# The latent feed-forward of a diffusion trunk by seven products of quarters, in two phases

## The chip, the cores and the metric

The kernel runs on one core of a Trainium2 chip. What is measured is the time of one execution on the device in microseconds (us). TensorE (PE) multiplies matrices from SBUF into PSUM, with weight loads (PEld) beside it; VectorE (DVE), ScalarE (ACT) and GpSimd (POOL) do the elementwise work; SyncE (SP) issues most DMA transfers, in one queue in order.

## What is computed

Two layers over 1024 latent tokens of 1024 features and 256 context tokens. Each layer has attention and pooling, an output projection with a layer norm, and then this feed-forward, whose result is added to the scaled input and normed again:

```python
def conv_ffn(h, w_up, conv_w, conv_b, w_down):
    u = h @ w_up
    L = u.shape[1]
    half = CONV_WIDTH // 2
    up = jnp.pad(u, ((0, 0), (half, half), (0, 0)))
    acc = up[:, 0:L] * conv_w[0] + conv_b
    for j in range(1, CONV_WIDTH):
        acc = acc + up[:, j:j + L] * conv_w[j]
    a, g = jnp.split(acc, 2, axis=-1)
    return (a * jax.nn.silu(g)) @ w_down

ffn = conv_ffn(x * (1 + s2) + sh2, w_up[l], conv_w[l], conv_b[l], w_down[l])
x = layer_norm(DEEPNORM_ALPHA * x + g2 * ffn, ln2_g[l], ln2_b[l])
```

All inputs are float32. In layer 0 the context tokens run the same feed-forward on their own; in layer 1 they don't.

## The kernel before

Every float32 operand of a large product is split into two float32r parts, a high one (a cast on ScalarE, `h`) and the rest (a subtraction on VectorE, `lo`). A product is three matmuls: high by high, high by low, low by high. A matmul here has 128 rows of contraction, 128 output rows and 512 columns. `wunit` (L149 on) loads 512 KB of weights into one of three `raw` buffers, casts (L156) and subtracts (L158).

The latent feed-forward is `ffn` (L1138 on) with the input `mixs`, which holds high and low parts of the tokens as `[128, 8 token tiles, 8 feature blocks, 128]`. It works on pairs f = 0 to 21 of blocks of 128 hidden features: `pair(f)` computes block f and block 22 + f. For one block `up` makes 2 halves of the tokens x 8 feature blocks x 3 = 48 matmuls (L1110). So there are 44 x 48 = 2112 matmuls a layer in the up product. `conv` (L1158 on) reads the block in PSUM: one activation on ScalarE for the middle tap, two `scalar_tensor_tensor` on VectorE for the others (L1163, L1166). Then SiLU on ScalarE (L1184), the gate as a product on GpSimd (L1185), and the split of the gated values.

The gated values stay in SBUF. After every two pairs (the list `G24`) `down` multiplies them by their rows of `w_down`, for 8 token tiles x 2 halves of the columns x 3 matmuls a pair (L1205), 1056 matmuls a layer in all. Before that GpSimd multiplies the raw weights by the gate vector `g2` (L154). VectorE adds each group's result into `acc` (L1216), a tile of 128 x 8 x 1024 in SBUF. `residual` (L1222 on) adds the scaled input in between: two products on GpSimd (L1226, L1227) and one `scalar_tensor_tensor` on VectorE (L1228). With the last group each token tile is normed (`ln_add`) and passed on by `tail`.

In layer 0 the background of the pairs also computes the next layer's modulation: 48 loads of 512 KB, each reduced by one VectorE instruction (L167). The first pair's products run ahead of the loop (`ups_before`), under the end of the output projection or of the context's feed-forward.

The program is written in this order, and a scheduler then sets the order of the instructions on each engine by its own estimate of times; each engine works off its row in order. PSUM is one pool of four tiles of 128 x 1024.

## Time and profile before

| what | value |
| --- | --- |
| median of 2 runs | 3015.48 us (3013.93 to 3017.04) |
| span of the profiled execution | 3008.6 us |
| TensorE matmuls | busy 2913.8 us (97%) |
| VectorE | busy 1872.5 us (62%) |
| ScalarE | busy 1261.9 us (42%) |
| GpSimd | busy 832.5 us (28%) |
| L1110, up, latent tokens | three groups of 1408 matmuls, 439 us each |
| L1205, down | three groups of 792 matmuls (264 of the 2376 belong to the context), 247 to 249 us each |
| DMA | 370.0 MB, 123 GB/s in the mean |

The span runs from the first to the last instruction on the core; the runs are timed from outside. Busy time is the union of the instructions of a group. Matmuls overlap one another, so the mean duration of one (389 ns) is not the distance between two; that distance comes out of a chain or a stretch. "Idle before" in a group is what the engine waited for ahead of it, and it costs something only on the engine that sets the end.

### The profile page before, as it was taken

Reading aid. Unit: us, or ns where it says so; the run is one execution under the profiler, and the core shown is the slowest. Engines: PE = TensorE matmul, PEld = TensorE weight load, DVE = VectorE, ACT = ScalarE, POOL = GpSimd, SP = SyncE. Lnnn points to the kernel's source line nnn. Section 1 sums busy time; section 2 is a strip of 40 time slices with the busy share of each in tenths; the row PEclk is TensorE's granted clock in tenths of the full one; section 3 lists DMA queues with packets and bytes.
Section 4 is the critical chain, followed back from the end, with each engine's and each line's share of the span. In section 5 each row is a group of like instructions: output and inputs, shape, how many; then the busy total and the mean of one; then the engine's idle time right before and its main releaser. Section 6 shows DMA issues by size and latency. Waiting matters only on the chain. (4 is left out here: it accounts for less than half of the span.)

```text
span 3008.6 us, 40753 instructions
## 1 busy us (share of the span) xinstructions
PE 2913.8 (97%) x15507; PEld 2477.8 (82%) x15507; DVE 1872.5 (62%) x3146; ACT 1261.9 (42%) x1980; POOL 832.5 (28%) x668
## 2 busy tenths in 40 slices
PE   8998889999999999999999999999999999999998
PEld 6798778977887888888888789888878888888886
DVE  5975789936886655556445754799845354444445
ACT  4223888834554322222223423798733322222223
POOL 0204363122532312121202632343222221212213
PEclk9999999999999999999999999999999999999999
DMA  7886652154554433332221654642133111211211
GB/s 282 246 271 188 186 162 89 36 175 164 177 187 155 159 98 98 106 111 91 84 63 64 211 191 141 176 126 87 57 117 112 57 50 49 63 56 56 70 46 60
DMA packets 186790, 370.00 MB, mean 123 GB/s; under 512 B 17290, under 2 KB 101346, under 8 KB 186084
## 3 DMA queue, kind: packets, MB, share of 16 engines
q1 hardware_dynamic: 185300, 363.11, 38.2%
q10 hardware_dynamic: 1296, 4.29, 0.4%
q8 instruction: 123, 2.02, 0.3%
q14 instruction: 71, 0.58, 0.1%
HBM read 303.46 MB, written 63.89 MB: 122 GB/s over the span
## 5 line engine op out<-in xcount | busy, mean ns | idle before, releaser
L158 DVE TENSOR_TENSOR wl<-raw,wh 128x1024 fp32r<-128x1024 f32 (+1 forms) x244 | 320.5, 1318 | 471.0 <-ACT wh L156 468.2
L156 ACT CAST wh<-raw 128x1024 fp32r<-128x1024 f32 (+1 forms) x250 | 258.2, 1037 | 824.2 <-PE u L1110 564.0
L1110 PE MATMUL u<-mxh,wh 128*128 128x512 f32 x1408 | 439.1, 390 | 2.6 <-DVE xtnl L163 1.5
L1110 PE MATMUL u<-mxl,wh 128*128 128x512 f32 x1408 | 439.0, 389 | 0.1
L1110 PE MATMUL u<-mxh,wl 128*128 128x512 f32 x1408 | 438.7, 389 | 0.0
L1110 PEld LDWEIGHTS u<-mxh,wh 128*128 128x128 f32 x1408 | 264.1, 188 | 58.1 <-DVE xtnl L163 1.7
L1110 PEld LDWEIGHTS u<-mxl,wh 128*128 128x128 f32 x1408 | 264.3, 188 | 55.6 <-DVE mxl L163 0.5
L1110 PEld LDWEIGHTS u<-mxh,wl 128*128 128x128 f32 x1408 | 264.3, 188 | 54.8
L154 POOL TENSOR_TENSOR raw<-raw,g 128x1024 f32<-128x1024 f32 x66 | 162.0, 2458 | 494.4 <-DMA raw<-in_wdown_dram 288.2
L163 DVE TENSOR_TENSOR PT<-pt,PT 128x512 fp32r<-128x512 f32 (+2 forms) x396 | 247.8, 644 | 17.4 <-ACT PT L162 14.9
L1205 PE MATMUL d<-wl,fh 128*128 128x512 f32 x792 | 249.1, 395 | 8.7 <-DVE wl L158 8.3
L1205 PE MATMUL d<-wh,fh 128*128 128x512 f32 x792 | 246.6, 395 | 2.7 <-ACT wh L156 1.3
L755 PE MATMUL s<-K,q 128*128 128x256 f32 (+2 forms) x960 | 235.5, 358 | 12.8 <-DVE m L722 11.2
L1205 PE MATMUL d<-wh,fl 128*128 128x512 f32 x792 | 247.7, 393 | 0.0
L1185 POOL TENSOR_TENSOR cv<-cv 128x1024 f32<-128x1024 f32 (+1 forms) x63 | 125.1, 1987 | 411.8 <-ACT cv L1184 411.8
L763 ACT ACTIVATE P<-P,m 128x1280 f32<-128x1280 f32 (+3 forms) x216 | 221.9, 1028 | 7.4 <-DVE m L722 6.4
L162 ACT CAST PT<-pt 128x512 fp32r<-128x512 f32 (+2 forms) x396 | 205.3, 558 | 24.2 <-PE pt L803 10.5
L817 PE MATMUL pvs<-PT,V 128*128 128x256 f32 (+1 forms) x1488 | 209.1, 288 | 5.1 <-DVE PT L163 2.0
L1216 DVE TENSOR_TENSOR acc<-d,acc 128x1024 f32<-128x1024 f32 x144 | 173.4, 1218 | 60.0 <-PE d L1205 59.9
L722 DVE CUSTOM_DVE_ANT_0 P<-s,zero,m 128x512 f32<-128x512 f32 (+1 forms) x288 | 189.0, 656 | 19.1
L299 PE MATMUL pacc<-wh,mxh 128*128 128x512 f32 (+1 forms) x512 | 189.4, 370 | 7.1 <-DVE rt L265 2.8
L817 PEld LDWEIGHTS pvs<-PT,V 128*128 128x128 f32 x1488 | 185.5, 190 | 11.8 <-ACT mixr L828 4.2
(237 smaller groups left out, 5449.2 us busy)
## 6 DMA issues: line engine op xcount, KB each, us to landing
raw<-in_wup_dram SPq DMA_DIRECT2D x132, 512.0 KB, 3.6
wm<-in_wmT_dram SPq DMA_DIRECT2D x96, 512.0 KB, 4.1
raw<-in_wdown_dram SPq DMA_DIRECT2D x66, 512.0 KB, 3.8
q<-QN SPq DMA_DIRECT2D x96, 128.0 KB, 3.3
q<-QG SPq DMA_DIRECT2D x96, 128.0 KB, 2.8
VD<-stB SPq DMA_DIRECT2D x20, 512.0 KB, 3.1
KD<-kt SPq DMA_DIRECT2D x20, 512.0 KB, 3.5
K<-KD SPq DMA_DIRECT2D x16, 640.0 KB, 5.0
```

The lines of the kernel that those rows point to most:

```text
L156: nc.scalar.copy(h[:, :n], raw[:, :n])
L158: (sub or nc.vector).tensor_tensor(out=lo[:, :n], in0=raw[:, :n], in1=h[:, :n], op=ALU.subtract)
L162: nc.scalar.copy(h, src)
L163: nc.vector.tensor_tensor(out=lo, in0=src, in1=h, op=ALU.subtract)
L299: nc.tensor.matmul(acc[:, :n], lhsT=xh[:, i, k, :], rhs=wh[:, o:o + n], start=(k == 0), stop=False)
L722: nc.vector.tensor_tensor_reduce(out=dst, in0=src, in1=bias, scale=-1.0, scalar=init, op0=ALU.add, op1=ALU.min, accum_out=m)
L755: nc.tensor.matmul(s[:, :n], lhsT=q[:, part, c0:c0 + P], rhs=K[:, k0:k0 + n], start=(part == 0), stop=(part == 1))
L763: nc.scalar.activation(out=self.P, in_=self.P, func=AF.Exp, bias=self.m, scale=-1.0, accum_out=self.rsum())
L817: nc.tensor.matmul(self.pv[:, c0:c0 + n], lhsT=V[:, vb, :], rhs=x[:, sl, c0:c0 + n], start=(self.c == 0), stop=(self.c == self.tot - 1),)
L1110: nc.tensor.matmul(o, lhsT=w, rhs=x, start=st, stop=sp)
L1205: nc.tensor.matmul(o[:, c], lhsT=x[:, tc_], rhs=w[:, c], start=(n_ == 0 and x is fh and w is wh), stop=(n_ == len(fs) - 1 and x is fl),)
L1216: nc.vector.tensor_tensor(out=s, in0=o, in1=s, op=ALU.add)
```

## The change

Both products of the latent feed-forward are cut into 2 x 2 quarters and computed by the Strassen-Winograd scheme: seven products of quarters and sums of quarters, in place of eight products. The up product and the down product become two phases. The context's feed-forward stays as it was.

Up (`UpLat`): the quarters are halves of the tokens by halves of the features, against halves of the contraction by the blocks f (`a`) and 22 + f (`g`) of the weights. `sum_x` forms three sums of the tokens' quarters once a layer, splits them into `T1`, `T2` and `T4` and writes the fourth, `T3`, over a quarter of `mixs`. For each pair `weights` forms four sums of weights on GpSimd (`s` in two halves, `ra` high half, `rg` low half) and splits `a`, `s4`, `s` and `g`. `P1` to `P7` are seven products of 4 x 3 = 12 matmuls; their results are combined in `u`, `ca` and `cg`, from PSUM and SBUF. `conv` then reads `ca` and `cg` in SBUF. `gate` forms the gated values; each second pair also four sums of quarters of them on GpSimd; all seven operands go to DRAM (`HD`, 256 KB each). Beside that `sum_w` loads two blocks of `w_down`, forms four sums on GpSimd and stores them (`TD`).

Down (`DownLat`): seven products of 11 units; a unit loads 256 KB from `HD` and 256 KB of weights or of `TD` into one `raw` buffer, is split as a whole, and makes 4 token tiles x 3 = 12 matmuls. The results are combined in `u` and `s` and scaled by `g2`; `finish` adds the residual and norms. A layer has 22 x 84 = 1848 matmuls in the up phase and 77 x 12 = 924 in the down phase. `acc` and `residual` into it are gone.

The core of the diff (comments and the last tile's special case left out):

```diff
+    def hl(pool, n, tags, src, **kw):
+        h = pool.tile([P, n], F32R, tag=tags[0], name="wh", **kw)
+        lo = pool.tile([P, n], F32R, tag=tags[1], name="wl", **kw)
+        split(h, lo, src)
+        return h, lo
+    class UpLat:
+        order = [x for j in range(NP) for x in (j, NP + j)]
...
+        def sum_x(self):
+            mx, xs, fu = self.mx, self.xs, self.fu
+            for t in range(4):
+                x1 = fu.tile([P, 1024], F32, tag="cv", name="x1", bufs=CVB)
+                x2 = fu.tile([P, 1024], F32, tag="cv", name="x2", bufs=CVB)
...
+                tt(nc.gpsimd, x1, flat(mx[0], t), flat(mx[1], t), ALU.add)
+                tt(nc.vector, x2, flat(mx[0], 4 + t), flat(mx[1], 4 + t), ALU.add)
+                lo, hi = slice(0, 512), slice(512, 1024)
+                tt(nc.vector, x1[:, lo], x2[:, lo], x1[:, lo], ALU.subtract)
+                tt(nc.gpsimd, x2[:, lo], x2[:, hi], x2[:, lo], ALU.subtract)
+                tt(nc.vector, x2[:, hi], x2[:, hi], x1[:, lo], ALU.subtract)
+                tt(nc.gpsimd, x1[:, hi], x1[:, hi], x2[:, hi], ALU.subtract)
...
+        def weights(self, f, first, third, rest):
+            ra = self.load(f, rawp, "raw")
+            if first:
+                b["a"] = hl(wp, 1024, ("wh", "wl"), ra)
+            rg = self.load(NF + f, self.fu, "rg", bufs=2)
+            s = self.fu.tile([P, 1024], F32, tag="s", name="s", bufs=1)
+            tt(nc.gpsimd, s[:, lo], rg[:, lo], rg[:, hi], ALU.add)
+            tt(nc.gpsimd, s[:, hi], s[:, lo], ra[:, lo], ALU.subtract)
+            if third:
+                tt(nc.gpsimd, ra[:, hi], ra[:, hi], s[:, hi], ALU.subtract)
+                b["s4"] = hl(self.fu, 512, ("w4h", "w4l"), ra[:, hi], bufs=1)
+            if rest:
+                tt(nc.gpsimd, rg[:, lo], ra[:, lo], rg[:, lo], ALU.subtract)
+                b["s"] = hl(wp, 1024, ("wh", "wl"), s)
+                b["g"] = hl(wp, 1024, ("wh", "wl"), rg)
...
+        def P5(self, f):
+            o = b["o2"][:, 512:1024]
+            self.mm(o, b["s"], 0, "T1", True)
+            cg = b["cg"] = self.fu.tile([P, 1024], F32, tag="Cg", name="Cg", bufs=1)
+            tt(nc.vector, cg[:, 512:], o, b["u"], ALU.add)
+            tt(nc.vector, b["ca"][:, 512:], b["ca"][:, 512:], cg[:, 512:], ALU.add)
...
+        def conv(self, C, f):
+            nc.scalar.activation(out=cv, in_=C, func=AF.Identity, bias=c[:, 3:4], scale=c[:, 1:2])
+            nc.vector.scalar_tensor_tensor(
+                out=cv[:, 1:T], in0=C[:, 0:T - 1], scalar=c[:, 0:1], in1=cv[:, 1:T], op0=ALU.mult, op1=ALU.add
+            )
...
+        def gate(self, f):
+            nc.scalar.activation(out=cg, in_=cg, func=AF.Silu)
+            tt(nc.gpsimd, ca, ca, cg, ALU.mult)
...
+            tt(nc.gpsimd, s3, ha[:, lo], ha[:, hi], ALU.subtract)
+            put("S3", s3)
+            tt(nc.gpsimd, ha[:, hi], ha[:, hi], hb[:, hi], ALU.add)
+            put("S1", ha[:, hi])
...
+        def sum_w(self, j):
+            w0 = rawp.tile([P, 1024], F32, tag="raw", name="w0")
+            nc.sync.dma_start(out=w0, in_=a["wdown"][l, j])
...
+            tt(nc.gpsimd, w0[:, lo], w0[:, hi], w0[:, lo], ALU.subtract)
+            tt(nc.gpsimd, w0[:, hi], w1[:, hi], w0[:, hi], ALU.subtract)
+            tt(nc.gpsimd, w1[:, hi], w1[:, hi], w0[:, lo], ALU.subtract)
+            tt(nc.gpsimd, w1[:, lo], w1[:, lo], w1[:, hi], ALU.subtract)
...
+        def run(self, ahead):
...
+                self.P6(f)
...
+                self.P5(f)
+                self.P7(f)
+                last = f
+                if g is not None:
+                    self.P1(g)
+                if g is not None or i + 1 == n:
+                    self.P4(f)
+                    self.gate(f)
+                    last = None
+                self.background(i)
+                if i % 2:
+                    self.sum_w(i // 2)
+                if g is not None:
+                    self.P3(g, self.blocks[g]["o1"])
+                    self.P2(g)
+    class DownLat:
+        products = (
+            ("A11", "B11"), ("S2", "T2"), ("A12", "B21"), ("S1", "T1"), ("S3", "T3"), ("S4", "B22"), ("A22", "T4")
+        )
...
+        def unit(self, p, j):
+            raw = rawp.tile([P, 1024], F32, tag="raw", name="hw")
+            nc.sync.dma_start(out=raw[:, 0:512], in_=HD[l, h][j])
...
+            nc.sync.dma_start(out=raw[:, 512:1024], in_=src)
...
+                return hl(wp if own < 0 else self.du, 1024, ("wh", "wl"), raw)
...
-                ffn(0, LAT, mixs, fl, ffp, ps, cols, g2l, bg_l, XS[0], lnrows, tail_l, ready)
+                up.enter(fu, quarters(xsp), bg_l)
+                up.sum_x()
+                up.run(AHEAD)
+            DownLat(0, ps, fd, du, g2).run(DU[0], DTAIL[0], finish_l)
```

How the rows of GpSimd stand in layer 1 before, for one group of two pairs (`raw<-raw,g` scales the down weights, `cv<-cv` is the gate, `xin` the residual):

```order
L154 TENSOR_TENSOR raw<-raw,g_22251 128x1024 x2
L1185 TENSOR_TENSOR cv<-cv 128x1024
L1226 TENSOR_TENSOR xin<-xin,lg 128x1024
L1227 TENSOR_TENSOR xin<-xin,lb 128x1024
L1185 TENSOR_TENSOR cv<-cv 128x1024
```

And after, in the up phase of layer 1, for about one and a half pairs (`s`, `raw` are sums of up weights, `w0`, `w1` of down weights, `cv` 128x1024 the gate, `s3` and `cv` 128x512 sums of gated values):

```order
L1269 TENSOR_TENSOR s_24618<-raw_24616 128x512
L1269 TENSOR_TENSOR w0_24727<-w1_24729,w0_24727 128x512
L1269 TENSOR_TENSOR s_24618<-s_24618,raw_24610 128x512
L1269 TENSOR_TENSOR raw_24616<-raw_24610,raw_24616 128x512
L1269 TENSOR_TENSOR w1_24729<-w1_24729,w0_24727 128x512
L1269 TENSOR_TENSOR w1_24729<-w1_24729 128x512
L1269 TENSOR_TENSOR cv_24572<-cv_24572,cv_24576 128x1024
L1269 TENSOR_TENSOR s3_24718<-cv_24572 128x512
L1269 TENSOR_TENSOR raw_24610<-raw_24610,s_24618 128x512
L1269 TENSOR_TENSOR s_24774<-raw_24772 128x512
L1269 TENSOR_TENSOR s_24774<-s_24774,raw_24766 128x512
L1269 TENSOR_TENSOR raw_24772<-raw_24766,raw_24772 128x512
```

The products of weights by `g` are gone, and sums of half width stand in their place, of three kinds in one row.

VectorE before, in the same part of layer 1 (`wl<-raw,wh` splits weights, `cv<-u,conv,cv` are the taps of the convolution from PSUM, `fl` splits gated values):

```order
L158 TENSOR_TENSOR wl<-raw,wh 128x1024 x2
L1163 SCALAR_TENSOR_TENSOR cv<-u,conv,cv 128x1023
L1166 SCALAR_TENSOR_TENSOR cv<-u,conv,cv 128x1023
L158 TENSOR_TENSOR wl<-raw,wh 128x1024
L1163 SCALAR_TENSOR_TENSOR cv<-u,conv,cv 128x1023
L1166 SCALAR_TENSOR_TENSOR cv<-u,conv,cv 128x1023
L163 TENSOR_TENSOR fl<-cv,fh 128x1024
L158 TENSOR_TENSOR wl<-raw,wh 128x1024
```

And after (`Cg<-o2` and `Cg<-o3` add from PSUM after P5, P7 and P4, `wl<-s` and the others split weights, `cv<-Ca` and `cv<-Cg` are the taps):

```order
L1269 TENSOR_TENSOR Cg_25531<-o2_25505,u_25427 128x512
L1269 TENSOR_TENSOR Ca_25453<-Ca_25453,Cg_25531 128x512
L171 TENSOR_TENSOR wl_25498<-s_25488,wh_25497 128x1024
L1269 TENSOR_TENSOR Cg_25531<-o3_25534,Cg_25531 128x512
L171 TENSOR_TENSOR wl_25493<-raw_25480,wh_25492 128x512
L1410 SCALAR_TENSOR_TENSOR cv_25576<-Ca_25453,conv_22156,cv_25576 128x1023
L1413 SCALAR_TENSOR_TENSOR cv_25576<-Ca_25453,conv_22156,cv_25576 128x1023
L1269 TENSOR_TENSOR u_25561<-o2_25661,u_25561 128x512
L1269 TENSOR_TENSOR Cg_25531<-o3_25534,u_25427 128x512
L171 TENSOR_TENSOR wl_25502<-raw_25486,wh_25501 128x1024
L1410 SCALAR_TENSOR_TENSOR cv_25580<-Cg_25531,conv_22156,cv_25580 128x1023
L1413 SCALAR_TENSOR_TENSOR cv_25580<-Cg_25531,conv_22156,cv_25580 128x1023
```

The taps now read `Ca` and `Cg` in SBUF, and the additions that the products wait for stand between splits and taps. In TensorE's row of this place the twelve matmuls of the next pair's P1 stand between P5 and the next P6, which needs `wl_25498`.

## Rows read from the trace of the kernel before

**Rows 1.** The page: length of the execution, and busy time of each engine.

```profile
span 3008.6 us, 40753 instructions
PE 2913.8 (97%) x15507; PEld 2477.8 (82%) x15507; DVE 1872.5 (62%) x3146; ACT 1261.9 (42%) x1980; POOL 832.5 (28%) x668
```

**Rows 2.** Stretches of 50 us; the second line names the columns, (x) counts instructions.

```profile
core 0: us, PE busy (x) PEld busy (x) DVE busy (x) ACT busy (x) POOL busy (x), PEclk, DMA share, GB/s
1200.00:1250.00 50.00, 50.00 (x221) 41.22 (x220) 32.84 (x33) 8.66 (x9) 11.97 (x5) 1.00 0.39 126
2700.00:2750.00 50.00, 50.00 (x220) 40.97 (x219) 24.09 (x20) 11.14 (x11) 9.58 (x4) 1.00 0.17 53
350.00:400.00 50.00, 40.86 (x288) 36.90 (x289) 38.58 (x125) 39.17 (x102) 27.78 (x46) 0.93 0.72 196
0.00:50.00 50.00, 42.81 (x314) 31.64 (x315) 20.61 (x60) 14.48 (x21) 3.60 (x8) 1.00 0.84 306
```

**Rows 3.** The chain that ended last in order of time: start us, us, what.

```profile
2357.94 43.57 PE u L1110 x192
2401.51 22.40 PE d L1205 x96
```

**Rows 4.** Instructions of single lines of code; the first line names the columns.

```profile
engine op xcount: duration ns min/median/max, first and last start us, forms
L158 DVE TENSOR_TENSOR wl<-raw,wh x244: 947/1225/3403, 35.0 to 2953.5; 128x1024 fp32r<-128x1024 f32 x114, 128x768 fp32r<-128x768 f32 x8
L1228 DVE SCALAR_TENSOR_TENSOR acc<-xin,acc x18: 1214/1226/3404, 773.4 to 2822.8; 128x1024 f32<-128x1024 f32 x18
L167 DVE CUSTOM_DVE_ANT_0 wm<-wm,ar,bmod x48: 1271/1285/3407, 978.3 to 1438.1; 128x1024 f32<-128x1024 f32 x48
L1185 POOL TENSOR_TENSOR cv<-cv x63: 737/2391/3386, 748.1 to 2937.1; 128x1024 f32<-128x1024 f32 x42, 128x256 f32<-128x256 f32 x21
L1185 DVE TENSOR_TENSOR cv<-cv x6: 279/692/693, 939.8 to 2959.5; 128x512 f32<-128x512 f32 x4, 128x128 f32<-128x128 f32 x2
```

**Rows 5.** Groups of GpSimd by line and shape: xcount | busy us, mean ns.

```profile
L614 POOL TENSOR_TENSOR mxl<-S,mxh 128x512 fp32r<-128x512 f32 x8 | 10.3, 1292 | 0.4
L680 POOL TENSOR_TENSOR S<-S 128x525 f32<-128x525 f32 x4 | 4.2, 1061 | 0.2
```

**Rows 6.** Timeline of VectorE, then GpSimd, 999 to 1026 us: start, us, engine, line.

```profile
999.43 2.46 DVE L158 TENSOR_TENSOR wl<-raw,wh 128x1024 fp32r<-128x1024 f32 x1 [2.29 <-ACT wh L156]
1016.40 1.28 DVE L1163 SCALAR_TENSOR_TENSOR cv<-u,conv,cv 128x1023 f32<-128x1023 f32 x1
1018.92 3.41 DVE L167 CUSTOM_DVE_ANT_0 wm<-wm,ar,bmod 128x1024 f32<-128x1024 f32 x1
1022.26 3.40 DVE L1228 SCALAR_TENSOR_TENSOR acc<-xin,acc 128x1024 f32<-128x1024 f32 x1
...
998.41 2.40 POOL L154 TENSOR_TENSOR raw<-raw,g 128x1024 f32<-128x1024 f32 x1
1000.77 3.38 POOL L1185 TENSOR_TENSOR cv<-cv 128x1024 f32<-128x1024 f32 x1
1015.29 3.47 POOL L1226 TENSOR_TENSOR xin<-xin,lg 128x1024 f32<-128x1024 f32 x1 [11.14 <-DMA xin<-XS]
1018.84 2.40 POOL L1227 TENSOR_TENSOR xin<-xin,B 128x1024 f32<-128x1024 f32 x1
1021.19 3.39 POOL L1185 TENSOR_TENSOR cv<-cv 128x1024 f32<-128x1024 f32 x1
```

**Rows 7.** Groups of ScalarE, 1000 to 2973 us; columns as in rows 5.

```profile
L156 ACT CAST wh<-raw 128x1024 fp32r<-128x1024 f32 x143 | 149.9, 1053 | 714.9 <-PE u L1110 554.3 <-PE d L1205 146.6 <-DMA raw<-in_wout_dram 8.3
L1162 ACT ACTIVATE cv<-u,conv 128x1024 f32<-128x1024 f32 x82 | 98.7, 1204 | 0.0
L1184 ACT ACTIVATE cv<-cv 128x1024 f32<-128x1024 f32 x41 | 43.5, 1061 | 148.6 <-DVE cv L1166 148.6
```

**Rows 8.** The page's DMA issues: xcount, size, median us to landing.

```profile
raw<-in_wdown_dram SPq DMA_DIRECT2D x66, 512.0 KB, 3.8
```

More of the change, by code (lines that the diff above doesn't have):

```diff
@@ L42 @@
 NST = 3
-TLAG = 4
+TLAG = 2
+AHEAD = 2
+DU = (3, 8)
+DTAIL = (6, 11)
 ENDC = 832
@@ L62 @@
 LNB = 4
+CVB = 3
 G34 = [2] * 8 + [3] * 2
@@ L1251, in right_pool, with quarters, scaled_rows, residual @@
         return st, st.enter_context(tc.tile_pool(name=name, bufs=bufs, side="right", reuse_waits="tile"))
+    def quarters(pool):
+        return [[pool.tile([P, 4, 4, P], F32R, name=f"{n}{x}") for x in "hl"] for n in ("T1", "T2", "T4")]
+    def scaled_rows(l, pool):
+        rows = [row_tile(pool, nm, a[nm][l]) for nm in ("ln1_g", "ln1_b")]
+        for r in rows:
+            nc.scalar.mul(r, r, ALPHA)
+        return rows
+    def residual(pool, x1, rows, t, tag="xin"):
+        x = pool.tile([P, D], F32, tag=tag, name="xin", bufs=2 if tag == "xin" and x1 is XS[1] else 1)
+        nc.sync.dma_start(out=x, in_=x1[t * P:(t + 1) * P, :])
+        tt(nc.gpsimd, x, x, rows[0], ALU.mult)
+        tt(nc.gpsimd, x, x, rows[1], ALU.add)
+        return x
     att = []
@@ new lines, in trunk_kernel, with bg_l @@
+                mods = list(range(48))
+                def bg_l(i):
+                    for j in [mods.pop(0) for _ in range(min(len(mods), 3 if i < 8 else 2))]:
+                        wm = load_wm(1, j, rawp, "raw")
+                        mod_tile(1, j, LAT, wm, ar1, wm)
+                    if i in (19, 20):
+                        GBl[i] = rows_begin(1, LAT, i == 19)
+                    if i in (20, 21):
+                        rows_end(1, LAT, ps, i == 20, *GBl[i - 1])
+                up.enter(fu, quarters(xsp), bg_l)
@@ L1474, in before_end @@
                 wx4s.close()
-                for x in ((xcs, wx1s) if XO else (wx1s, xcs)):
+                for x in (wx1s, xcs):
                     x.close()
```

395 lines of the change are left out of this document (310 added, 85 removed).

## Prediction

> **What bounds the kernel now.** I read the page's busy shares first: TensorE is busy 97% of the span, no other engine over 62% [rows 1]. Then the stretches of 50 us inside the two latent feed-forwards: TensorE 50.00 of 50.00 us, VectorE 24 to 33, ScalarE 9 to 11, GpSimd 10 to 12, granted clock 1.00 [rows 2]. Then the chain that ended last, which inside layer 1 is nothing but TensorE: 192 matmuls of the up product in 43.57 us (0.2269 us each), 96 of the down product in 22.40 us (0.2333 each) [rows 3]. So a latent feed-forward costs its matmuls: up 2112 x 0.2269 = 479.2 us, down 1056 x 0.2333 = 246.4 us, per layer. Everything else is cover. The chain for layer 0 is not printed, but its stretch reads the same.
>
> **What is taken away.** Seven products for eight: up 2112 to 1848 matmuls, down 1056 to 924. If TensorE stayed dense: up 479.2 to 419.3 (-59.9), down 246.4 to 215.6 (-30.8), two layers -181.4 us. The 64 additions a layer of a down group into `acc` on VectorE go too; they lay under matmuls and are worth nothing by themselves.
>
> **What is added to the other engines, and where it lies.** In the up phase a layer has these instructions with two inputs in SBUF.
> GpSimd, 512 wide: 24+24+22+22 sums of weights (the first two pairs form two of them twice), 44 sums for the down weights, 44 sums of gated values, 8 of the tokens' sums: 188. GpSimd, 1024 wide: 22 gates, 4 of the tokens' sums: 26. The nearest row for a 512-wide one is 1.292 us, for a 1024-wide one 2.391 [rows 4, 5]: 242.9 + 62.2 = 305.1 us.
> VectorE, 1024 wide: 66 splits of weights, 88 convolution taps (they now read SBUF, where they read PSUM before), 4 token sums: 158 at 1.225, the two-SBUF median of L158 and L1228 [rows 4]. 512 wide: 22 splits, 22 sums into `Ca`, 24 for the tokens: 68 at 0.692 [rows 4]. Together 193.6 + 47.1 = 240.6 us. Layer 0 also has the 48 reductions of the next modulation, 1.285 each [rows 4]: 61.7.
> The four additions from PSUM a pair are VectorE's as well, but have one SBUF input.
>
> Now the rows that decide. At 1018.92 a VectorE reduction that lasts 1.285 alone takes 3.41 us: GpSimd's L1227 runs from 1018.84 to 1021.24, and VectorE ends 1.09 after it. The next VectorE instruction, at 1022.26, takes 3.40 where 1.226 is usual, behind GpSimd's L1185, which itself took 3.39 because VectorE was in front of it [rows 4, 6]. At 1016.40 the convolution tap that reads PSUM takes its 1.28 us while GpSimd runs L1226 all through [rows 6]. So instructions of the two engines with two SBUF operands exclude each other; one with a PSUM operand is free. The time of such instructions therefore adds up over both engines: 305.1 + 240.6 = 545.7 us in layer 1's up phase and 607.4 in layer 0's, against 419.3 of matmuls. Before, the same two engines left TensorE dense because GpSimd had 10 to 12 us of work in 50 [rows 2]; now GpSimd alone needs 305.
>
> What a change of hands saves: GpSimd ends at 1000.81, VectorE's 1.225 us instruction at 1001.89, GpSimd's next at 1004.15: 3.34 us for a pair whose parts alone make 3.61, so 0.27 less [rows 6]. With 214 GpSimd instructions a layer, each meeting VectorE once at 0.27, that is at most 57.8 us: 487.9 and 549.6. Below that the phase can only come if the token sums start under the output projection and the last gate ends under the down phase: one conv (2 x 1.226 + 1.204), SiLU, gate and sums are about 13 us, say 15 [rows 4, 7]. Nothing says how often hands change, and both queues are in order, so that at times neither has its operands. One such place is in the order shown: VectorE must add P5, add into `Ca` and split the next `s` (0.69 + 0.69 + 1.225 = 2.6 us) while TensorE has one product, 12 x 0.2269 = 2.7 us; each of the two SBUF ones can stand behind a GpSimd sum of 1.29. I take the middle of the bounds, half the saving: 545.7 - 28.9 = 516.8 and 607.4 - 28.9 = 578.5, together 1095.3. TensorE then idles 98 and 159 us in the two phases.
>
> The Trainium skill, "SBUF — State Buffer", section "Who interferes with whom", has it that the engine that issues first gets the shared pair of ports for the whole instruction and the other one fully blocks. By that there is no saving at a change of hands, and the up phases would take 545.7 and 607.4. Rows 6 show 0.27 us saved per pair, so I keep the rows' bound in the sum and the rule as a rival.
>
> **The rest of the edits.** ScalarE has per pair three casts of 1.05, two activations of 1.20, a SiLU of 1.06 and four pieces of 512 at some 0.6, half a cast: 9 us in a step of 19 or more [rows 7]; nothing. Transfers: a pair moves 1.0 MB of up weights, 0.5 of down weights, 0.5 of their sums, 0.9 of gated values and in layer 0 1.1 of modulation: 4.0 MB in about 26 us, 155 GB/s; the down phase 512 KB per 12 matmuls (2.8 us), 187 GB/s. The start of the kernel moved 306 GB/s at a share of 0.84 [rows 2], so I take nothing. If it were late: three `raw` buffers, 3.8 us of landing [rows 8] plus cast 1.05 and split 1.225 make 6.1 us, 2.0 per unit against 2.8. The stores stand in SP's queue ahead of later loads and wait for GpSimd, so a late sum delays the next weights as well; this only follows GpSimd and is in the step already. In the down phase VectorE has 1.225 per unit of 2.8 and GpSimd almost nothing, so down is TensorE's 215.6. At its 12 changes of product one eviction of 0.69 can be open [rows 4]: 0 to 10 us; I take 10, for the first units after the up phase, too.
>
> **Sum.** Up 1095.3 - 958.4 = +136.9; down -61.6; changes +10: +85.3. The profiled span is 3008.6 us, the median of the runs 3015.5; the difference of 7 us I leave alone. 3015.5 + 85.3 = 3101 us.
>
> **Rivals.**
> - Exclusion at its cheapest: every change of hands saves, head and tail are covered: up 472.9 + 534.6 = 1007.5, +49.1 - 51.6 = -2.5: 3013 us. For it: both queues are long, so hands may change at each instruction. Against: in-order queues.
> - Other side, faster: GpSimd's sums of halves run like L680's 128x525 at 1.061 [rows 5], not 1.292. 188 x 0.231 = 43.4 a layer off the rival above: up 920.7, 2926 us. It decides from the point where both up phases take under 950 us together (the 2% line). Against: L680's operands lie in one tile a few columns apart, the new sums' in separate tiles or halves, like L614's.
> - Exclusion for whole instructions, no saving: up 1153.1, 3159 us. For: layer 0's queue is full.
> - The change does what it says: the waits fall into slack, up 419.3 each: -119.8 - 51.6: 2844 us. Against: 545.7 us do not fit in 419.3 if they exclude each other.
> - TensorE's clock falls: with gaps of some us in each step. In the stretch at 350 us, TensorE busy 40.86 of 50, it was 0.93 [rows 2], that is 7 us at 1.2 GHz, 3.5 us lost. One such loss in every second of 44 steps adds 77: 3178 us.
>
> **How the numbers follow.** Forecast 0.36 (own range 3040 to 3160), cheap exclusion 0.22, fast sums 0.12, whole instructions 0.15, as it says 0.08, clock 0.07. The predicted time is the forecast's, 3101. The range leaves out the last two (0.15): 2915 to 3180. Faster by over 2% (about what a measurement of this kernel can tell from no change: below 2955): fast sums and as it says, 0.20. Within 2%: the cheap exclusion and 0.08 of the forecast, 0.30. Slower (above 3076): 0.50.
>
> **What would show it.** In the up phases: time per pair near 23.5 us in layer 1 and 26.3 in layer 0 (19.1 would be matmuls alone); the taps in SBUF well over 1.23 us in the mean and GpSimd's 512-wide sums over 1.29; TensorE at 73 to 81%, waiting for VectorE's splits and additions. In the down phases: TensorE dense, about 216 us. Wrong, if up takes under 440 us a layer with both engines' sums above it, or if the down phase is over 230 us, or if the loss sits in loads (then the cost is SP's queue, not the exclusion).

## The result, and the profile after

The changed kernel takes 3245.98 us (median of 3244.24 and 3247.72) against 3015.48: a ratio of 1.0768, 95% interval 1.0737 to 1.0799. The direction was forecast; the size was not: 3245.98 lies 66 us above the upper end of the range, and 145 above the forecast. The page of the profiled execution, span and busy time of each engine, to set beside [rows 1]:

```profile
span 3242.5 us, 41789 instructions
...
PE 2833.6 (87%) x14715; PEld 2365.3 (73%) x14715; DVE 2415.5 (74%) x3475; ACT 1484.3 (46%) x2288; POOL 1504.4 (46%) x1030
```

TensorE has less to do (2833.6 us against 2913.8), VectorE 543 us more and GpSimd 672 us more of busy time, in which waiting for each other is counted.

Where the stages begin and end is read from the first and last start of the matmuls of three lines: L1305 is the up phase (`o`), L1534 the down phase (`dx`), L307 the next layer's projection (`pacc`). Columns: count, duration min/median/max in ns, first and last start in us.

```profile
L1305 PE MATMUL o<-mxh,wh x352: 387/389/796, 946.2 to 1549.2; 128*128 128x512 f32 x176
...
L1534 PE MATMUL dx<-wh x176: 387/389/793, 1549.9 to 1777.5; 128*128 128x512 f32 x176
...
L1534 PE MATMUL dx<-wh,wl x176: 389/389/628, 1551.4 to 1778.9; 128*128 128x512 f32 x176
...
L307 PE MATMUL pacc<-wh,xtch x32: 389/389/793, 1825.9 to 1863.4; 128*128 128x512 f32 x32
...
L1305 PE MATMUL o<-mxh,wh x352: 387/389/774, 2441.9 to 2964.4; 128*128 128x512 f32 x176
...
L1534 PE MATMUL dx<-mxh,mxl x128: 388/389/628, 2980.0 to 3202.3; 128*128 128x512 f32 x128
...
L1534 PE MATMUL dx<-wh x48: 388/389/632, 2967.9 to 3196.4; 128*128 128x512 f32 x48
```

Layer 0's up phase thus runs from 946.2 to 1549.9, its down phase to 1778.9; the projection starts 47.0 us later, at 1825.9. Layer 1's up phase runs from 2441.9 to 2967.9, its down phase to 3202.3, and 40.2 us of the span are left after that. In the trace of before, read in the same way, the feed-forwards run from 941.6 to 1670.4 and from 2266.4 to 2995.4, the projection starts at 1673.8, and the end is 3008.6:

```profile
L1110 PE MATMUL u<-mxh,wh x704: 387/389/504, 941.6 to 1622.9; 128*128 128x512 f32 x176
...
L1205 PE MATMUL d<-wh,fl x376: 388/389/398, 913.2 to 1670.4; 128*128 128x512 f32 x188
...
L299 PE MATMUL pacc<-wh,xtch x32: 387/391/628, 1673.8 to 1705.8; 128*128 128x512 f32 x32
...
L1110 PE MATMUL u<-mxh,wh x704: 387/389/499, 2266.4 to 2949.7; 128*128 128x512 f32 x176
...
L1205 PE MATMUL d<-wh,fl x352: 389/393/399, 2336.3 to 2995.4; 128*128 128x512 f32 x176
```

| stage, us | before | forecast | after | after - forecast |
| --- | --- | --- | --- | --- |
| up to layer 0's up phase | 941.6 | 941.6 | 946.2 | +4.6 |
| layer 0: up | 479.2 | 578.5 | 603.7 | +25.2 |
| layer 0: down | 246.4 | 220.6 | 229.0 | +8.4 |
| from there to the projection | 3.4 | 3.4 | 47.0 | +43.6 |
| projection, attention, output projection | 592.6 | 592.6 | 616.0 | +23.4 |
| layer 1: up | 479.2 | 516.8 | 526.0 | +9.2 |
| layer 1: down | 246.4 | 220.6 | 234.4 | +13.8 |
| end | 13.2 | 13.2 | 40.2 | +27.0 |

(Up and down of before are the products of counts and distances in the prediction; they come out 7 us shorter than the two feed-forwards of its trace. The forecast's 10 us for changes of product are halved between the down phases.) So the column on the right adds up to 155 us, of which those 7 are no miss. Nearly half of it, 71 us, lies right behind the two down phases, where no term of the sum stood; 34 in the up phases, 22 in the down phases, 23 in the stretch from the projection to the output projection.

Stretches of the profile after (columns in the first line), to set beside [rows 2]:

```profile
core 0: us, PE busy (x) PEld busy (x) DVE busy (x) ACT busy (x) POOL busy (x), PEclk, DMA share, GB/s
1200.00:1250.00 50.00, 42.46 (x174) 32.89 (x173) 48.78 (x36) 17.94 (x21) 38.23 (x18) 0.97 0.55 172
2700.00:2750.00 50.00, 47.27 (x200) 36.69 (x199) 42.17 (x31) 20.59 (x24) 42.67 (x22) 1.00 0.45 142
3130.00:3180.00 50.00, 50.00 (x222) 41.42 (x221) 29.54 (x31) 18.04 (x18) 16.11 (x10) 1.00 0.47 147
955.00:1005.00 50.00, 14.89 (x56) 10.50 (x55) 38.56 (x33) 14.86 (x22) 34.30 (x20) 0.66 0.37 125
2480.00:2520.00 40.00, 15.02 (x49) 11.55 (x48) 27.93 (x22) 7.51 (x12) 24.25 (x15) 0.62 0.26 85
```

In the middle of an up phase TensorE is busy 42 and 47 us of 50. At its start (955 and 2480) it is busy 15 of 50 and of 40 us, at a granted clock of 0.66 and 0.62 (a mean over time at 2.4 and at 1.2 GHz, behind gaps of 19 to 25 us), while VectorE and GpSimd form the sums of the tokens. In the down phase it is dense: 222 matmuls in 50.00 us, 0.2252 each.

The work for one pair of blocks f is called a step here; an up phase has 22. VectorE in the middle of layer 1's up phase, by line: count, busy us, mean ns, then its idle time.

```profile
L1410 DVE SCALAR_TENSOR_TENSOR cv<-Ca,conv,cv 128x1023 f32<-128x1023 f32 x14 | 31.9, 2280 | 1.1 <-ACT cv L1409 1.1
L1413 DVE SCALAR_TENSOR_TENSOR cv<-Ca,conv,cv 128x1023 f32<-128x1023 f32 x14 | 30.4, 2173 | 0.5
L171 DVE TENSOR_TENSOR wl<-s,wh 128x1024 fp32r<-128x1024 f32 x14 | 26.9, 1922 | 0.0
...
L1269 DVE TENSOR_TENSOR Cg<-o,u 128x512 f32<-128x512 f32 x28 | 19.1, 684 | 1.6 <-PE o L1305 0.3
```

And GpSimd in the same stretch:

```profile
L1269 POOL TENSOR_TENSOR raw<-raw 128x512 f32<-128x512 f32 x14 | 32.2, 2297 | 0.0
...
L1269 POOL TENSOR_TENSOR w<-w 128x512 f32<-128x512 f32 x14 | 22.9, 1634 | 2.4 <-DMA w<-in_wdown_dram 1.9
```

The taps on `Ca` take 2173 and 2280 ns in the mean (those on `Cg` 1685 and 1794) where a two-SBUF instruction of that size takes 1225 [rows 4], the splits of `s` 1922, GpSimd's sums of 512 columns in these two groups 1634 and 2297 where L614 took 1292 [rows 5]. The additions that read PSUM take 684: they are not touched. What [rows 6] had shown in two places now shows in the means of these groups.

### The profile page after: what moved, and what is told of

It reads as the page before. It is cut to its first block, busy times and chain, and to the rows that moved or that the text cites. A ratio compares the mean times of both kernels' runs of the same rounds, so it can differ in the third digit from the quotient of the medians.

```text
span 3242.5 us, 41789 instructions
## 1 busy us (share of the span) xinstructions
PE 2833.6 (87%) x14715; PEld 2365.3 (73%) x14715; DVE 2415.5 (74%) x3475; ACT 1484.3 (46%) x2288; POOL 1504.4 (46%) x1030
## 5 line engine op out<-in xcount | busy, mean ns | idle before, releaser
L1305 PE MATMUL o<-mxh,wl 128*128 128x512 f32 x704 | 285.1, 406 | 41.8 <-DVE wl L171 41.8
L1305 PE MATMUL o<-mxh,wh 128*128 128x512 f32 x704 | 282.1, 404 | 27.3 <-ACT wh L170 24.9
L1269 POOL TENSOR_TENSOR cv<-cv 128x512 f32<-128x512 f32 (+1 forms) x110 | 240.6, 2188 | 134.7 <-ACT cv L1422 114.1
L1305 PE MATMUL o<-mxl,wh 128*128 128x512 f32 x704 | 282.7, 402 | 0.0
L763 PE MATMUL s<-K,q 128*128 128x256 f32 (+2 forms) x960 | 236.1, 359 | 13.4 <-DVE m L730 12.0
L171 DVE TENSOR_TENSOR wl<-hw,wh 128x1024 fp32r<-128x1024 f32 x98 | 130.2, 1335 | 93.1 <-ACT wh L170 92.4
L1305 PEld LDWEIGHTS o<-mxh,wl 128*128 128x128 f32 x704 | 136.8, 194 | 83.4 <-DVE wl L171 53.5
L307 PE MATMUL pacc<-wh,mxh 128*128 128x512 f32 (+1 forms) x512 | 190.7, 372 | 4.5 <-DVE rt L273 1.7
L308 PE MATMUL pacc<-wl,mxh 128*128 128x512 f32 (+1 forms) x512 | 187.0, 365 | 0.0
L309 PE MATMUL pacc<-wh,mxl 128*128 128x512 f32 (+1 forms) x512 | 186.4, 365 | 0.0
L1305 PEld LDWEIGHTS o<-mxh,wh 128*128 128x128 f32 x704 | 137.5, 195 | 59.5 <-ACT wh L170 26.2
L170 ACT CAST wh<-hw 128x1024 fp32r<-128x1024 f32 x98 | 102.8, 1052 | 149.6 <-PE dy L1534 34.6
```

Of the source, the lines that this page charges most:

```text
L170: nc.scalar.copy(h, src)
L171: nc.vector.tensor_tensor(out=lo, in0=src, in1=h, op=ALU.subtract)
L307: nc.tensor.matmul(acc[:, :n], lhsT=xh[:, i, k, :], rhs=wh[:, o:o + n], start=(k == 0), stop=False)
L308: nc.tensor.matmul(acc[:, :n], lhsT=xh[:, i, k, :], rhs=wl[:, o:o + n], start=False, stop=False)
L309: nc.tensor.matmul(acc[:, :n], lhsT=xl[:, i, k, :], rhs=wh[:, o:o + n], start=False, stop=(k == 7))
L763: nc.tensor.matmul(s[:, :n], lhsT=q[:, part, c0:c0 + P], rhs=K[:, k0:k0 + n], start=(part == 0), stop=(part == 1))
```

## Experiments

Each time stands beside 3011.4 to 3016.5 us of the kernel before on the same chip. Where no ratio is given it is one execution; the others are medians of 4 to 7.

### What sets the up phases

Theories: the exclusion of VectorE and GpSimd (the forecast's), the transfers and their queue, VectorE's own row.

**Sums of the down weights left out, with and without their transfers.**

```diff
-tt(nc.gpsimd, w0[:, lo], w0[:, hi], w0[:, lo], ALU.subtract)    # and three more; transfers stay
```


> The 88 GpSimd sums of halves of the down weights (44 a layer, 512 wide) are left out; their two loads and four stores a group stay, so the down products get unsummed quarters. If the exclusion of VectorE and GpSimd sets the up phases, 88 x 1.29 us = 114 us of a time that is added up go; less what a change of hands had saved (at most 0.27 each, 24 us): 3246 - 90 to 114 = 3132 to 3156 us, the up phases 45 to 57 us shorter each (from 610 and 534 us). If instead the queue of transfers (SP's loads and stores behind each other) sets the up phases, the same bytes move and the time stays within 15 us of 3246.


```diff
-if i % 2:
-    self.sum_w(i // 2)                                           # the transfers go too
```


> As the run before, and the loads and stores of those weights in the up phases are left out too (22 x 2 loads of 512 KB and 22 x 4 stores of 256 KB in all); the down phase reads quarters of the weights as they stand in memory. If the exclusion is what counts, the up phases take what they take in the run without sums, within 10 us together. If transfers or their place in SP's queue hold the up phase, another 30 us or more go.

3164.76 and 3169.99 us. 81 us go with 88 sums, a little less than the exclusion's 90 to 114, and nothing more goes with the transfers. The up phases are 43 and 31 us shorter, where 45 to 57 each were expected. So the transfers of the weights' sums do not hold the phase. That it is less than the sums' own time shows that order counts as well: two steps of the steady part of layer 1 go from 42.9 to 40.9 us, where the summed time of the two engines goes from 45.4 to 40.2.

**Everything on VectorE.**

```diff
-tt(nc.gpsimd, ...)      # the 16 calls in UpLat
+tt(nc.vector, ...)
```


> All 214 two-operand instructions that GpSimd has in an up phase go to VectorE, nothing is left out. If the two engines exclude each other, the sum of their times is what counts: per layer 188 x 0.692 + 26 x 1.225 = 162 us on VectorE in place of 305 on GpSimd; VectorE then has 193.6 + 47.1 + 162 + 88 additions from PSUM of 0.685 = 463 us in layer 1, 525 in layer 0, and nobody to wait for: the up phases take about 475 and 537 us in place of 534 and 610, 3246 - 132 = 3114 us (3090 to 3150). If VectorE's own row sets the phase and GpSimd runs beside it, 162 us come on top in each: about 3570. If transfers set it, 3246.

3099.73 us, 146 less, and the up phases 530.6 and 463.8 us by the same reading. VectorE takes over 214 instructions a layer and the phase gets shorter: a row of its own cannot have been the bound, nor the transfers, which are the same. A stretch of layer 1 in the columns of the stretches above, and a tap there, by line as above:

```profile
2600.00:2650.00 50.00, 50.00 (x218) 40.57 (x217) 45.26 (x55) 23.83 (x28) 0.00 (x0) 1.00 0.45 146
```
```profile
L1410 DVE SCALAR_TENSOR_TENSOR cv<-Ca,conv,cv 128x1023 f32<-128x1023 f32 x16 | 20.5, 1280 | 5.9 <-ACT cv L1409 5.8
```

The same tap that took 2280 ns beside GpSimd takes 1280 without it. GpSimd does nothing, VectorE 45 us of 50, and TensorE is dense again, at 38.8 us for two steps (168 matmuls). In layer 0, with the modulation, VectorE is the bound (49.58 of 50 us at 1200). The same work takes less on one engine than on two. The exclusion says so, and it was helped by VectorE being faster at it: a sum that took GpSimd 1.292 us alone takes VectorE 0.692.

**GpSimd with one operand.**

```diff
+def one(out, a_, b_):
+    nc.gpsimd.tensor_copy(out=out, in_=a_)
-tt(nc.gpsimd, x, y, z, op)
+one(x, y, z)
```


> Each of GpSimd's 214 two-operand instructions of an up phase becomes a copy of its first operand on GpSimd (same length, same place, same order; the values are then wrong). If only instructions with two operands in SBUF exclude each other, VectorE's taps, which took 2.2 to 2.3 us in the phase, fall back to 1.23, VectorE then needs 301 us in layer 1, and layer 1's steady step falls from 21.45 us to TensorE's 19.3: up phases near 475 and 545 us, 3120 us in all (3100 to 3150), whatever a GpSimd copy takes as long as it is under about 1.7 us. If any work of GpSimd on SBUF keeps VectorE out, the taps stay above 2 us and the time stays within 40 us of 3246.

3074.93 us: below both expectations (3100 to 3150, or within 40 of 3246), and not for the reason given. A stretch of the timeline, VectorE, then GpSimd:

```profile
2606.85 0.69 DVE L1269 TENSOR_TENSOR Cg<-o,u 128x512 f32<-128x512 f32 x1 [0.72 <-PE o L1308]
...
2617.19 1.62 DVE L1413 SCALAR_TENSOR_TENSOR cv<-Cg,conv,cv 128x1023 f32<-128x1023 f32 x1
...
2606.75 0.62 POOL L1272 COPY s<-cv 128x512 f32<-128x512 f32 x1
...
2617.68 1.61 POOL L1272 COPY s<-s 128x512 f32<-128x512 f32 x1
```

A copy of 512 columns takes 0.62 us beside an addition from PSUM (2606.75, 2606.85). The one at 2617.68 takes 1.61: it ends 0.48 after the tap of 2617.19, which itself takes 1.62 behind the copy before it. So a copy with one SBUF operand is kept out as well, and keeps VectorE out; the step is fast because a copy alone is half as long as a sum: the summed time of the two engines for two steps is then some 32 us, under the 38.7 that TensorE takes in this run. My sentence "two SBUF operands" was too narrow on GpSimd's side. The Trainium skill, "SBUF — State Buffer", section "Who interferes with whom", says of this that a VectorE instruction with two SBUF inputs contends with a GpSimd instruction that reads SBUF; the trace agrees with it.

### Why layer 0 is longer than layer 1

```diff
-mod_tile(1, j, LAT, wm, ar1, wm)
+mod_tile(1, j, LAT, wm[:, 0:16], ar1[:, 0:16], wm[:, 0:16])
```


> The 48 reductions for the next layer's modulation, which run in layer 0's up phase, read 16 of 1024 columns; their loads stay whole (the modulation is then wrong in value). Summed time of the two engines: 48 x (1.285 - about 0.15) = 54 us less in layer 0's up phase, none in layer 1's: layer 0's up from 610 to about 556 us, 3192 us in all, whether it is the exclusion or VectorE's own row that binds. If loads bind layer 0's up phase, it stays at 610.

3224.14 us: a miss. Layer 0's up phase fell by 17 us (603.7 to 586.2), not by 54. VectorE's waits in the phase from 1050 to 1450 us (sum us, times, longest), of the changed kernel and of this one:

```profile
DVE wm L175 <- DMA wm<-in_wmT_dram: 13.6, 11, 7.7
```
```profile
DVE wm L175 <- DMA wm<-in_wmT_dram: 62.5, 11, 9.0
```

What the reductions no longer took, VectorE waited for their loads. These share a ring of three buffers (three tiles that are filled in turn, each free only when its last reader is done) with the up weights and with halves that GpSimd sums in place.

```diff
-wm = load_wm(1, j, rawp, "raw")
+wm = rawp.tile([P, 1024], F32, tag="raw", name="wm")
+nc.sync.dma_start(out=wm[:, 0:16], in_=a["wmT"][1, j][:, 0:16])
```


> The 48 modulation tiles of layer 0's up phase are loaded and reduced over 16 of 1024 columns (one load of 8 KB for each of 512 KB). With the reductions alone cut, the phase had still taken 594 us, and VectorE had waited 62 us in 400 for these loads. If the loads and their place in the ring of three buffers are what keeps layer 0 above layer 1, its step falls from 25.2 us to layer 1's 21.5 and a little: up near 550 us, 3186 us in all (3175 to 3200). If it is something else that layer 0 has, it stays near 594 and 3224.

3179.88 us, and the up phase 551.9: as expected. So two bounds lie close together in layer 0: the exclusion (reductions) and behind it late loads. Loads were not cut alone, so the runs do not tell their bytes from their place in the ring; and 27 us by which the phase is still longer than layer 1's 524.5 in this run were not followed up.

### Each half by itself

```diff
-up.sum_x(); up.run(AHEAD)        # seven products
+up.run(AHEAD)                    # eight products of whole blocks, as in ffn
```


> One part alone: the up phase forms all eight products again (2112 matmuls a layer, no sums of tokens or weights, VectorE's taps read PSUM); gated values and their sums still go through memory, and the down phase keeps its seven products. GpSimd then has 88 sums of 1.29 us and 22 gates of 2.4 in a phase of 479 us of matmuls, VectorE nothing that fills it. If the exclusion made the up phases long, TensorE is dense again: about 487 us each, from 610 and 534; down phases 222 and 226 and the ends 47 and 40 as they were: 3246 - 170 = 3076 us (3060 to 3095). If the traffic through memory or SP's queue made them long, up stays over 520: 3150 and more.

3115.06 us, 131 less, 39 short of the expectation. Two stretches, of layer 0 and layer 1:

```profile
1200.00:1250.00 50.00, 46.20 (x202) 37.30 (x200) 22.80 (x22) 11.13 (x11) 17.32 (x11) 1.00 0.52 165
2400.00:2450.00 50.00, 50.00 (x223) 41.40 (x222) 15.33 (x13) 10.79 (x11) 17.20 (x11) 1.00 0.40 132
```

Layer 1 is as expected, dense, 483 us. Layer 0 took 523 (950.1 to 1473.4), which is 36 of the 39: VectorE waits there for the loads of the modulation, and TensorE behind it for split weights.

```profile
DVE wm L175 <- DMA wm<-in_wmT_dram: 143.5, 36, 13.4
```

In the kernel before, the same loads had up and down in turn, about 33 us a step ((479.2 + 246.4) / 22), to come in; with the two phases apart they have 22. That this is why they come late is argued, not tested.

### The ends of the phases

The changed kernel between the layers, VectorE, then GpSimd (start, us):

```profile
1809.60 1.21 DVE L225 CUSTOM_DVE_ANT_0 s<-xin,s 128x1024 f32<-128x1024 f32 x1
...
1814.74 2.29 DVE L239 TENSOR_TENSOR lnb<-lnm,lrs 128x1 f32<-128x1 f32 x1 [0.67 <-POOL lrs L235]
1820.81 3.35 DVE L246 TENSOR_TENSOR xm<-xm,B 128x1024 f32<-128x1024 f32 x1 [3.79 <-POOL xm L245]
1824.08 1.21 DVE L225 CUSTOM_DVE_ANT_0 s<-xin,s 128x1024 f32<-128x1024 f32 x1
...
1814.67 2.34 POOL L1269 TENSOR_TENSOR xin<-xin,ln_g 128x1024 f32<-128x1024 f32 x1
1818.44 2.34 POOL L245 TENSOR_TENSOR xm<-s,G 128x1024 f32<-128x1024 f32 x1 [1.43 <-ACT s L240]
1820.74 2.34 POOL L1269 TENSOR_TENSOR xin<-xin,ln_b 128x1024 f32<-128x1024 f32 x1
```

TensorE waits in this gap for the finished tiles (us in all, times, longest; `xm` is the normed tile on its way to the next projection):

```profile
PE tps L251 <- DVE xm L246: 39.2, 4, 12.6
```

A token tile takes 14.48 us (1809.60 to 1824.08, the two L225). GpSimd has three instructions of 2.34 in it (residual times `ln_g`, plus `ln_b`, and the product with `G`), VectorE's `xm` addition takes 3.35 behind one of them, and an `lnb` of 128x1 takes 2.29 behind another. `xin` is one buffer, so the next residual's load waits for the L225 of this one. In the kernel before, the residual of a tile was made between two down groups ([rows 6] show one, L1226 and L1227, at 1015, 655 us ahead of the end of the feed-forward).

```diff
+ahead(4 + t, s[4 + t])          # in c22: load, two GpSimd instructions and an addition, by halves
-x = residual(fd, XS[0], lnrows, t)
```


> Of the last token tiles of the down phase (four in layer 0, three in layer 1) the residual (a load and two GpSimd instructions of 2.4 us) is made two products earlier, by halves; VectorE adds the upper half there, and only the lower half is left for the end. If the 47 us behind layer 0's down phase and the 40 us behind layer 1's are the finish of these tiles one behind the other (14.5 us a tile, of which 4.8 and more are the residual behind one buffer), the step of a tile falls to about 8 us: 20 to 25 us less between the layers, 10 to 15 at the end, 3246 - 35 = 3211 us (3200 to 3222). If instead the next projection waits for its own weights, and the end for its stores, nothing changes: 3246.

3210.80 us, the expected 3211. The gap between the layers fell from 47.0 to 36.2, the end from 40.2 to 25.0, and the projection (the matmuls of L307 to L309) from 213.0 to 203.9. The same diff on top of two others, the sums on VectorE and the eight products:

> Both edits at once: all sums of the up phases on VectorE (3099.7 us by itself) and the residual of the last tiles ahead. The ends of the phases took 47.8 and 40.2 us with the sums on VectorE too, so the two gains add: 3100 - 35 = 3065 us (3055 to 3077). If the ends are set by something else, 3100.

3071.89 us.

> Eight products up, seven down, and the residual of the last tiles ahead. If both theories hold, the gains add: 3076 - 35 = 3041 us (3025 to 3060), against 3016 of the kernel before: seven down products save 2 x 22 us, and what is left of the late ends and the two separate phases costs more than that. If the ends are not the residual, 3076.

3083.77 us: the gain adds to the other two nearly as expected (28 and 31 us of 35). The second time still misses its range of 3025 to 3060, by what the eight products alone had missed.

```diff
+ahead(t, s[t], hi, sums[t][:, 0:1])        # in c11, the other four tiles as well
-... perm, True, mul=nc.gpsimd)
+... perm, True, mul=nc.vector)             # layer 0
```


> All sums of the up phases on VectorE, and in the down phase the residual of all eight token tiles ahead of their last product, by halves (before: of the last four in layer 0 and three in layer 1), the multiplication by G in layer 0 on VectorE. If the ends are the finish of the tiles one behind the other, the gap behind layer 0's down phase falls from 36 us (47.8 without any of it) to about 15, the end from 25 (40.2) to about 20: 3072 - 26 = 3046 us (3035 to 3060). If the gap is set by the next projection's weights, it stays: 3072.

3030.18 us, 16 better than expected: the gap is 25.9 us now, not 15, the end 13.4 (13.2 in the kernel before). So the end was the finish of the tiles, and 21 of the 47 us between the layers as well. What is left of the gap is the norm of the last four tiles, which all come out of the last product: TensorE waits there for a tile's variance (`lve`) and for `xm`. This is read from the trace; no run takes it away.

```profile
PE tps L254 <- DVE lve L236: 11.1, 1, 11.1
PE tps L254 <- DVE xm L249: 8.1, 2, 4.2
```

### The start of an up phase

```diff
-tt(nc.gpsimd, x1, flat(mx[0], t), flat(mx[1], t), ALU.add)      # and the five others of a tile
```


> The six sums of the tokens' quarters per tile are left out at the start of each up phase; the splits behind them stay (of unsummed quarters, so the values are wrong). By their rows they are 4 x (2.391 + 1.225 + 2 x 0.692 + 2 x 1.292) = 30.3 us of a summed time of 41 us. If the 50 us that the first steps of an up phase take beyond the later ones are these sums, 25 to 30 us go in each layer: 3246 - 55 = 3191 us (3180 to 3205). If the first steps wait for the last token tiles of the output projection or for the first weights, less than 10 us go in all: over 3235.

3195.75 us, 50 less: layer 0's up phase is 32 us shorter (571.5) and layer 1's 25 (501.4; layer 0's began 7 us later in this run). Nothing covers the token sums. In layer 1 the first four steps are 33 us shorter (106 for 139), but the steady part, in which nothing was changed, is slower: 44.3 us for two steps in place of 42.9.

### Layer by layer

```diff
-up = UpLat(0, mixs, ps, uf, cols)          # and what hangs on it
+ffn(0, LAT, mixs, fl, ffp, ps, cols, g2l, bg_l, XS[0], lnrows, tail_l, ready)
```


> Layer 0's latent feed-forward as in the kernel before (eight products, up and down in turn), layer 1's exactly as changed. By the accounting of the stages layer 1's part of the loss is 31 us in the feed-forward, 27 at the end and 12 in the output projection ahead of it: 3012 to 3015 + 70 = 3084 us (3074 to 3096), and the other 160 of the 231 us are layer 0's with the step to the next layer. If the two layers' losses are not separate (a lower clock, a shared stall), it misses that by over 20 us.

3077.62 us, within the expected range: layer 1's part is 64 us by itself, the other 166 are layer 0's with what lies between the layers. The losses are separate.

The same layer 0, and in layer 1 the sums on VectorE and the finish ahead:

> Layer 0's latent feed-forward as in the kernel before; layer 1 with seven products, all its sums on VectorE and the residual of its tiles ahead. Layer 0 with those two edits still took 771 us from its up phase to the next projection, against 732.5 before; layer 1 with them takes 710.5 us to the end against 742 before. So 3030 - 39 = 2991 us (2980 to 3003), some 0.7% faster than the kernel before (3011 to 3015). If the gain of layer 1 hangs on something in layer 0, 3015 or more.

2992.68 us, as expected; ratio to before 0.9931 (0.9918 to 0.9943). This is the fastest version. It beats the kernel before by less than the 2% that the prediction counted as a difference, but its interval lies below 1; so do those of its two variants with other rings below. Its page:

```profile
span 2992.8 us, 41264 instructions
...
PE 2840.3 (95%) x15111; PEld 2412.0 (81%) x15111; DVE 2134.2 (71%) x3543; ACT 1373.0 (46%) x2134; POOL 770.4 (26%) x645
```

**Modulation under the output projection.**

```diff
-mods = list(range(48))
+mods = list(range(24, 48))                 # the first 24 ahead of the output projection's norms; the others two, then one a step
```


> As the run before, and 24 of the 48 modulation reductions of layer 0's up phase lie under layer 0's output projection, where VectorE had 12 us of work in 50. VectorE is the bound of layer 0's up phase there (21.7 us a step): 24 x 1.285 = 31 us less in it, none more in the projection, whose matmuls fill TensorE: 3046 - 31 = 3015 us (3000 to 3035), even with the kernel before. If their loads hold up the projection's own, the projection loses what the phase gains: 3046.

3035.71 us, ratio 1.0080 (1.0064 to 1.0097): a miss. The up phase did lose 33 us (492.1 for 525.4), but the output projection grew from 125 to 161: TensorE waited there for VectorE's `xm`, behind reductions that came at the pace of their loads.

```profile
PE tps L254 <- DVE xm L249: 38.2, 4, 31.6
```

**A ring of its own for the down phase.**

```diff
-raw = rawp.tile([P, 1024], F32, tag="raw", name="hw")
+raw = fd.tile([P, 1024], F32, tag="raw", name="hw", bufs=6)      # layer 1
```


> As the run before, and layer 1's down phase loads its units into six buffers of its own in place of the three that all loads share. An eviction there waited 8.3 us behind nine splits that came at 2.5 us each, at the pace of the loads; with loads ahead they come at VectorE's 1.23. If the ring sets the pace, the down phase falls from 226 to about 214 us: 2991 - 12 = 2979 us (2972 to 2985). If memory itself is the limit (299 to 415 GB/s in the first 40 us there), it stays at 2991.

3003.46 us, ratio 0.9976 (0.9963 to 0.9989): slower than without it. The down phase took 223 us from its first matmul, not 235.5, but began late (TensorE's wait, us):

```profile
PE dx L1538 <- ACT wh L170: 23.8, 1, 23.8
```

```diff
-pool, kw = (self.fd, dict(bufs=6)) if l else (rawp, {})
+pool, kw = (self.fd, dict(bufs=6)) if l and self.n > 7 else (rawp, {})
```


> As layer0_as_before, and layer 1's down phase loads its first eight units through the ring of three that all loads share, the others through six buffers of its own. With all units in its own ring the phase took 223 us from its first matmul to the last in place of 235.5, but began 24 us later, since its first loads stood in SP's queue behind the last gate's stores and the rows. If the pace of the ring is what stretched the phase, 12 us go without that late start: 2993 - 12 = 2981 us (2975 to 2987). If the first eight units are what is slow, nothing goes: 2993.

3002.50 us, ratio 0.9961 (0.9948 to 0.9975): a miss. TensorE now stood still for 12.4 us from 2759.2, where the first unit of the new ring was due. SP's queue there (start, us in the queue):

```profile
2754.51 1.74 SPq L1430 DMA_DIRECT2D HD1A<-cv  x2
2756.34 2.13 SPq L1430 DMA_DIRECT2D HD1S<-cv  x3
2758.53 0.45 SPq L218 DMA_DIRECT2D g<-rows1lat  x1
...
2761.21 0.49 SPq L1519 DMA_DIRECT2D hw<-HD1A  x1
```

The loads stand in SP's queue behind the last gate's stores, which are issued up to 2758.5, and behind the five rows of the down phase. Whether the ring paces the down phase is not settled. It took 12.5 us less in the first run, but there its loads could land during the 23.8 us before it began; in the second it took 245.3, or 232.9 without the standstill, only 2.6 less than 235.5. What the queue's order takes, 23.8 and 12.4 us, is shown, and it is more than the ring gave.

## Why the prediction was wrong

**What bounds the kernel now; what is taken away.** Right: in the middle of the down phase TensorE is dense again. Matmuls even come at 0.2252 us there, so a dense down phase would be 208 us, not 215.6.

**Exclusion, and what a change of hands saves.** Right as a mechanism, and in the steady part right in size. Two steps in layer 1 have 16 sums of 1.292, two gates of 2.391, fourteen 1024-wide instructions of 1.225 and four of 0.692: 45.4 us. From one copy of P1's result (`u<-o`) to the next but one it took 42.8 to 42.9, seven times in a row; here one of them:

```profile
2626.56 0.57 ACT L1361 COPY u<-o 128x512 f32<-128x512 f32 x1
...
2669.45 0.57 ACT L1361 COPY u<-o 128x512 f32<-128x512 f32 x1
```

That is 2.5 us saved of at most 18 x 0.27 = 4.9, half of it, as I had taken. By the rule of the Trainium skill, "SBUF — State Buffer", section "Who interferes with whom" (the whole instruction), it would have been 45.4; the trace does not agree with that, nor with the cheapest exclusion (40.5). That it is just half is chance: I took the middle of two bounds without a reason for it. The run without the token sums has the same instructions in its steady part and took 44.3, so 1.1 saved; without the weights' sums the period was 40.9, above its sum of 40.2. So the order of the two rows counts beside the exclusion, and how it does was not tried.

**The sum of the up phases** was 34 us short. In layer 1, 9: the first four steps take 139 us where four later ones take 86. The forecast had the tokens in its summed time, at 41 us with their splits, as if this were work like the rest; it had no term for a start that nothing covers, and the 15 us for head and tail stood only in the cheap rival, as a gain. 33 of the 53 us go with the token sums (the run without them); the clock falls to 0.62 there; the rest was not tried. In layer 0, 25: a step takes 25.2 us in the mean, from the fifth on, where half the saving gives 24.3 (45.4 / 2 + 61.7 / 22 - 9 x 0.27 / 2). VectorE waits there for the modulation's loads (13.6 us in 400), and 62.5 in 400 once the reductions are cut. "If it were late" stood in the prediction for the down weights alone, and for bandwidth I took nothing. The share of the DMA engines is 0.55 in that stretch, where the kernel's start had 0.84 [rows 2], which speaks for the ring and its users rather than for bandwidth; no run tells the two apart.

**"The rest of the edits"** is the step that failed. The finish of the eight token tiles was not in it. The diff took the residual out of the down groups and put it into `finish`; on GpSimd, one buffer, four tiles one behind the other after the last product. The edit had moved two instructions of 2.4 us and a load for each tile out of cover, and I priced the evictions alone ("0 to 10 us; I take 10") and left the two stretches behind the down phases as they were. They grew by 43.6 and 27.0 us. With the finish of all eight tiles ahead, 21.1 and 26.8 of that are gone, which is shown; the other 22.5 between the layers are the norms of the same tiles by TensorE's waits, which no run took away. Without these 71 us the time would have been some 3175, just inside the range. The 23 us between the projection and layer 1's up phase are in part the same: the projection took 213.0, with the residual ahead 203.9 and 199.0; but runs that leave the finish alone have 206.7 to 213.0, so between 3 and 9 us are the finish's. Another 12 are one gap of TensorE in layer 1's output projection (at 2366), which stands in the run with layer 1 alone changed too (at 2202). It waits there for `xm` of L246 (11.6 us; 2.2 in the kernel before); why that comes later was not tried.

**Down phases** took 229.0 and 234.4, "over 230" in one of them. In layer 1 one eviction waited behind nine splits, where the prediction had 0.69 us for each change of product:

```profile
PE dx L1534 <- DVE s L1269: 8.3, 1, 8.3
```

Loads that come late through the shared ring are one reading of it, which the two runs with a ring of its own leave open. So of the 22 us missed in the down phases this one wait of 8.3 is located, and its cause is not shown.

**Rivals.** None of them is it: the forecast's own case came out in the steps, and terms of the sum were missing. Clock: in the steady part it is 0.97 to 1.00, and it is low at the starts and behind the down phases. The granted clock of the whole span is 0.948 in the mean, 0.993 before, which by the two levels is about 340 us at 1.2 GHz in place of 42; what that costs where TensorE has work no run shows. The clock rival's 3178 also lay inside the range that was said to leave it out. Whole instructions would have given 3159, still too low without the ends. **What would show it:** steady steps 21.5 and 25.2 us (forecast 23.5 and 26.3 with the token sums spread over them), taps and sums long, TensorE 85 to 95% in the steps rather than 73 to 81: much of the idle time lies at the starts and the ends.

## What to carry to other kernels

Before giving work to a second engine, add up both engines' SBUF instructions: here VectorE alone was 146 us faster than VectorE and GpSimd that exclude each other. When a loop is cut into two phases, list for every helper of the old loop what it did between the groups, and price it at its new place without cover, with its buffers. Here the saving of matmuls paid only in the stage where the other engines had slack: in layer 1 alone, with its sums on one engine and the finish ahead, it gave 0.7%.

## What the runs showed of the hardware

I had not expected that a GpSimd copy with one SBUF operand is held up by VectorE's two-operand instructions as well: 0.62 us beside an instruction that reads PSUM, 1.61 beside a tap. Even an instruction of 128x1 on VectorE took 2.29 us behind a GpSimd product of 1024 columns (0.16 alone). And two engines that exclude each other settled into a strict period here: 42.9 us for two steps, with half the possible saving at the changes of hands, and 44.3 for the same work after another start.
